# Early bias loads moved to another queue and place, constant products ahead of the first projection, and two blocks of squares issued later, in a two-layer hybrid decoder trunk

## The chip, the cores and the metric

The kernel runs on one core of one Trainium2 chip. The metric is the device time of one execution in microseconds; lower is better. Engines are named as in the profile: PE is TensorE's matrix products, PEld its weight loads, DVE is VectorE, ACT ScalarE, POOL GpSimd, SP SyncE, which issues most of the DMA transfers.

## The reference

Input x is (1, 256, 2048) float32, and so is the output. Two layers; each is a mixer and a SwiGLU feed-forward, both with an RMS norm ahead and a residual add behind; a final RMS norm follows. Weights are float32.

```python
def reference(x, ...):
    h = x
    for layer in range(2):
        xn = rms_norm(h, norm_mix[layer])
        if layer % 2 == 0:
            # one projection feeds two groups of heads: sliding-window attention
            # (16 q heads, 4 kv heads of 64, window 128, ALiBi, sinks) and
            # mLSTM (4 heads, input gate and forget gate with biases b_i, b_f)
            mix = swa_mlstm_mixer(xn, w_in_even, w_out_even, swa_sinks, mlstm_b_i, mlstm_b_f, head_gain)
        else:
            # causal attention with 16 heads of 128 and a cumulative log forget gate (bias fox_b_f)
            mix = forgetting_attention_mixer(xn, w_in_odd, fox_b_f, w_out_odd)
        h = h + mix
        h = h + swiglu(rms_norm(h, norm_ffn[layer]), w_gate[layer], w_up[layer], w_down[layer])
    return rms_norm(h, norm_final)

def rms_norm(x, g):
    return x * lax.rsqrt(jnp.mean(x * x, axis=-1, keepdims=True) + 1e-5) * g
```

## The kernel before, in words

**Products.** Every float32 operand of a large product is split into a rounded part and a rest: `hi` and `lo` for weights, `xh` and `xl` (or `mh` and `ml`) for activations, which stand transposed, with the model dimension on the partitions. One product is then three: `hi` with `xh`, `lo` with `xh`, `hi` with `xl` (lines 184 to 186 in `gemm`, 405 to 407 in `three`).

**Weights** come in chunks of 256 rows by up to 512 columns: `load_raw` issues the transfer on SyncE's queue (line 112), into one of four buffers; `split_chunk` rounds it to `hi` on ScalarE (line 156) and subtracts on VectorE for `lo` (line 157). A chunk feeds 12 products: two slices of 128 rows, two tiles of 128 tokens, three parts. `latest[0]` is the last cast, `load[0]` the last load issued. `tc.issue_after(ins)` puts all that is issued inside it behind `ins` on that engine's queue. Apart from that, the order on each engine's queue is planned when the kernel is built, by the order in the source and by when the planner expects operands to be there; each engine then works through its queue in order.

**The start.** SyncE's queue loads the transposed input `xc` (five transfers, line 122), interleaved with the first four weight chunks of k's projection, `ahead`. Pool writes constants (`ident`, `ones`, `upper`, `mhalf`) and issues four small loads, each a row of 4 or 16 floats copied to all 128 partitions: `bias_g` (lines 140 and 141), `sink` (143), `bias_f` (145). The tiles are read much later: `sink` in the attention of layer 0, `bias_g` at the mLSTM's gates, `bias_f` at layer 1's gates.

The first projection is k and v of the sliding-window attention (eight chunks): ScalarE makes `xh` from `xc` with the norm's gain (line 689), VectorE `xl` (line 690), four slices at a time, then `gemm` runs over them. The norm's division is applied behind the product, by `r`. Then comes q's projection, eight chunks more, in four steps; with each step a quarter of the input `h` is loaded on SyncE's queue (line 700) and its squares summed on ScalarE (`square_sum`, line 207), for `r`.

**The seam from layer 0 to layer 1.** The feed-forward's last two output blocks (n = 2 and 3 of four blocks of 512 columns) are added to `h` by `close`; each is then turned for layer 1 in two steps that wait in the list `pending`. `start` issues a transposing DMA of the two halves of the words, `join` puts the halves together again (line 240, ScalarE), scales them to `xh` (line 262, ScalarE) and makes `xl` (line 263, VectorE). `first_values` runs the first products of layer 1 meanwhile, those that need only blocks 0 and 1 (k below 8, into `vacc0` and `tacc1`), then those of block 2 (k = 8 and 10), and takes a step from `pending` after four of them: both starts, the first join, and after `(0, 10)` the second. The squares of all four blocks, under the key `"m1"`, are summed in `close`, and `rstd("m1")` (lines 213 and 214 on VectorE, 216 on Pool) makes the norm's factor `r1` from them; it is first applied at line 1028.

Of the kernel before, what the change touches and what calls it, by code (L numbers as in the profile page):

```python
# [7 lines left out]
F32 = mybir.dt.float32  # L8
# [9 lines left out]
P = 128  # L18
# [14 lines left out]
OFF_QM, OFF_KM, OFF_VM, OFF_OM = 1536, 2048, 2560, 3584  # L33
CAP = 15.0
FILL = 24
ORDER = ((0, 0), (0, 1), (1, 2), (0, 3), (1, 4), (0, 5), (1, 6), (0, 7))
DOWN = {
    6: ((0, 0), (0, 1), (1, 2), (0, 3), (1, 4), (0, 5)),
# [14 lines left out]
def mixed_of(order):  # L53
    return [p for w, p in order if w]
# [5 lines left out]
def trunk(  # L60
# [20 lines left out]
    nc = tc.nc  # L81
# [8 lines left out]
    cp = ctx.enter_context(tc.tile_pool(name="cp", bufs=1))  # L90
    sm = ctx.enter_context(tc.tile_pool(name="sm", bufs=2))
    fill = ctx.enter_context(tc.tile_pool(name="fill", bufs=1)).tile([P, FILL], F32, name="fill")
    nc.gpsimd.memset(fill[:, 0:8], 0.0)
    pa = ctx.enter_context(tc.tile_pool(name="pa", bufs=4, space=PSUM))
    pm = ctx.enter_context(tc.tile_pool(name="pm", bufs=4, space=PSUM))
# [12 lines left out]
    load = [None]  # L108

    def load_raw(w, k0, c0, n, pool=wr, bufs=4):  # L110
        raw = pool.tile([P, CK, NB], F32, tag="raw", name="raw", bufs=bufs)
        load[0] = nc.sync.dma_start(
            raw[:, :, 0:n], w[k0 * P : (k0 + CK) * P, c0 : c0 + n].rearrange("(k p) n -> p k n", p=P)
        )
        return raw
# [5 lines left out]
    for k0, k1, ks in ((0, 2, (0,)), (2, 4, (2,)), (4, 8, (4, 6)), (8, 12, ()), (12, 16, ())):  # L121
        nc.sync.dma_start(xc[:, k0:k1, :], xt[:, k0:k1, :])
        ahead += [load_raw(wi, k, OFF_KS, NB) for k in ks]

    ident = cp.tile([P, P], F32, name="ident")
    nc.gpsimd.memset(ident, 0.0)
    nc.gpsimd.affine_select(
        out=ident, in_=ident, pattern=[[-1, P]], compare_op=ALU.not_equal, fill=1.0, base=0, channel_multiplier=1
    )
    ones = cp.tile([P, P], F32, name="ones")  # L130
    nc.gpsimd.memset(ones, 1.0)
    upper = cp.tile([P, P], F32, name="upper")
    nc.gpsimd.affine_select(
        out=upper, in_=ones, pattern=[[1, P]], compare_op=ALU.is_ge, fill=0.0, base=0, channel_multiplier=-1
# [2 lines left out]
    nc.gpsimd.memset(mhalf, -0.5)  # L137

    bias_g = cp.tile([P, 8], F32, name="bias_g")
    nc.gpsimd.dma_start(bias_g[:, 0:4], mlstm_b_i[0].partition_broadcast(P))  # L140
    nc.gpsimd.dma_start(bias_g[:, 4:8], mlstm_b_f[0].partition_broadcast(P))
    sink = cp.tile([P, SWA_H], F32, name="sink")
    nc.gpsimd.dma_start(sink, swa_sinks[0].partition_broadcast(P))
    bias_f = cp.tile([P, FOX_H], F32, name="bias_f")
    nc.gpsimd.dma_start(bias_f, fox_b_f[0].partition_broadcast(P))

    latest = [None]

    def load_chunk(w, k0, c0, n):
        raw = ahead.pop(0) if ahead else load_raw(w, k0, c0, n)  # L150
        return split_chunk(raw, n)
# [10 lines left out]
    def new_acc():  # L162
        return [pa.tile([P, NB], F32, tag="acc", name="acc") for _ in range(NT)]
# [6 lines left out]
    def gemm(acc, lhs, w, c0, n, k_from, k_to, k_all, skew=1):  # L170
        k0 = k_from
        while k0 < k_to:
            last = k_to == k_all and k0 + skew * CK >= k_all
            chunks = [load_chunk(w, kc, c0, n) for kc in range(k0, k_all if last else k0 + CK, CK)]
            order = [(i, t) for i in range(len(chunks) * CK) for t in range(NT)]
            if last:
                order.sort(key=lambda it: it[1])
            for i, t in order:
                k = k0 + i
                hi, lo = (c[:, i % CK, 0:n] for c in chunks[i // CK])  # L180
                ah, al = lhs(k)
                ts = slice(t * P, (t + 1) * P)
                o = acc[t][:, 0:n]
                nc.tensor.matmul(o, ah[:, ts], hi, start=(k == 0), stop=False)  # L184
                nc.tensor.matmul(o, ah[:, ts], lo, start=False, stop=False)  # L185
                nc.tensor.matmul(o, al[:, ts], hi, start=False, stop=(k == k_all - 1))  # L186
            k0 += len(chunks) * CK
# [14 lines left out]
    def square_sum(key, n):  # L202
        if n == 0:
            sums[key] = sm.tile([P, NT, 4], F32, tag="ss", name="ss")
        for t in range(NT):
            junk = sm.tile([P, NB], BF16, tag="junk", name="junk", bufs=1)
            nc.scalar.activation(
                junk, h[:, t, n * NB : (n + 1) * NB], AF.Square, accum_out=sums[key][:, t, n : n + 1]
            )
# [34 lines left out]
    def turn_scaled(room, idx, n, extra=None):  # L244
# [10 lines left out]
        def join():  # L255
# [10 lines left out]
            for half in range(2):  # L266
                pair = 2 * n + half
                if extra is None or pair not in mixed_of(ORDER):
                    continue
                m = mixed_of(ORDER).index(pair)  # L270

# [13 lines left out]
    def add_out(acc, n):  # L285
        for t in range(NT):
            o = h[:, t, n * NB : (n + 1) * NB]
            nc.vector.tensor_tensor(out=o, in0=acc[t], in1=o, op=ALU.add)
# [88 lines left out]
    def run_next(pending):  # L377
        if pending:
            with tc.issue_after(latest[0].ins):
                pending.pop(0)()  # L380
# [162 lines left out]
    def ffn(layer, fp, room, pending, sx, sd, key, idx_next=None, key_next=None, finish=None, then=None):  # L543
        r = rstd(key)

        def sums_x(pair):
            j = mixed_of(ORDER).index(pair)
            return sx[0][:, j, :, :], sx[1][:, j, :, :]

        for g0, g1 in zip(PARTS, PARTS[1:]):  # L550
# [5 lines left out]
            for g in range(g0, g1):  # L556
                par = (g1 - 1 - g) % 2
                plain, c = pair_group(
                    room, par, x_of, sums_x, [(w_gate[layer], g * NB), (w_up[layer], g * NB)], ORDER, todo
                )  # L560
# [60 lines left out]
            def close(acc, n):  # L621
                if not end:
                    add_out(acc, n)
                elif idx_next is None:
                    finish(acc, n, gf)
                else:
                    add_out(acc, n)
                    pending.extend(turn_scaled(room, idx_next, n))
                    square_sum(key_next, n)

            gf = None
            wd = w_down[layer][4 * g0 * P : 4 * g1 * P, :]
            for n0 in (0, 2):
                if end and idx_next is None and n0 == 2:
                    for n in (2, 3):
                        acc = new_acc()
                        gemm(acc, m_of, wd, n * NB, NB, 0, nk, nk, skew=3 if n == 3 else 1)
                        close(acc, n)
                    continue
# [22 lines left out]
                for m in range(2):  # L662
                    close(plain[m], n0 + m)
# [32 lines left out]
    acc1 = new_acc()  # L696
    for n in range(4):
        gemm(acc1, x_of, wi, OFF_QS, NB, 4 * n, 4 * n + 4, KT)
        with tc.issue_after(load[0].ins):
            nc.sync.dma_start(h[:, :, n * NB : (n + 1) * NB], xv[:, :, n * NB : (n + 1) * NB])  # L700
        square_sum("m0", n)
    r = rstd("m0")
    with tc.tile_pool(name="ev", bufs=1) as ev:
# [101 lines left out]
        acc = tacc  # L805
# [199 lines left out]
    late = ctx.enter_context(tc.tile_pool(name="late", bufs=1))  # L1005
    sx = [late.tile([P, len(mixed_of(ORDER)), 4, P], F32R, name=f"sx{i}") for i in range(2)]
    wi1 = w_in_odd[0]
# [7 lines left out]
    def first_values(pending):  # L1015
        for acc, c0, n, k0 in FIRST_ODD:
            gemm((vacc0, tacc1)[acc], x_of, wi1, c_v + c0, n, k0, k0 + 2, KT)
            if (acc, k0) in ((0, 4), (0, 6), (1, 4), (0, 10)):
                run_next(pending)

    close_layer(0, w_out_even[0], 2, "f0", begun=begun0, idx_next=1, key_next="m1", then=first_values)

    r1 = rstd("m1")
    with tc.tile_pool(name="od", bufs=1) as od:
# [8 lines left out]
        acc = tacc1  # L1033
# [120 lines left out]
    def finish(acc, n, gf):  # L1154
        ns = slice(n * NB, (n + 1) * NB)
        gn_ = gf[n // CK][:, n % CK, :]
        for t in range(NT):
            o = h[:, t, ns]
            nc.vector.tensor_tensor(out=o, in0=acc[t], in1=o, op=ALU.add)
            junk = sm.tile([P, NB], BF16, tag="junk", name="junk", bufs=1)  # L1160
            nc.scalar.activation(junk, o, AF.Square, accum_out=fs[:, t, n : n + 1])
            part, mean, rs = (ft[:, a, t : t + 1] for a in range(3))
            if n < 3:
                nc.vector.tensor_tensor(out=o, in0=o, in1=gn_, op=ALU.mult)
            if n == 2:
                nc.vector.reduce_sum(part, fs[:, t, 0:3], axis=AX)
                nc.vector.tensor_scalar(part, part, 1.0 / D, EPS, op0=ALU.mult, op1=ALU.add)
            if n < 3:
                continue
            nc.vector.tensor_scalar(mean, fs[:, t, 3:4], 1.0 / D, part, op0=ALU.mult, op1=ALU.add)  # L1170
            nc.gpsimd.tensor_tensor(out=rs, in0=mean, in1=mhalf[:, 0:1], op=ALU.pow)
            nc.scalar.mul(h[:, t, 0 : 2 * NB], h[:, t, 0 : 2 * NB], rs)
            nc.vector.tensor_scalar(h[:, t, 2 * NB : 3 * NB], h[:, t, 2 * NB : 3 * NB], rs, None, op0=ALU.mult)
            nc.vector.scalar_tensor_tensor(out=o, in0=o, scalar=rs, in1=gn_, op0=ALU.mult, op1=ALU.mult)
            for half in (1, 0):
                hs = slice(half * 2 * NB, (half + 1) * 2 * NB)
                nc.sync.dma_start(ov[:, t, hs], h[:, t, hs])
# [51 lines left out]
```

## Time and profile before

| | |
|---|---|
| median of 3 runs | 2106.6 us (2105.95 to 2106.67) |
| the profiled execution's own time | 2107.07 us |
| its span | 2105.4 us |
| granted TensorE clock, mean | 0.998 |
| TensorE (PE) busy | 99% of the span, 9558 products |
| VectorE, ScalarE, Pool busy | 86%, 63%, 2% |
| DMA | 429.33 MB, mean 204 GB/s |

The profile is one execution, and the times in it are microseconds from the start of its span. Idle time of an engine says what it waited for. A DMA share of 1 means that all 16 DMA engines are full.

### The profile page before, as it was taken

What the parts mean: (1) busy time and instruction counts of PE and PEld (TensorE: products, weight loads), DVE (VectorE), ACT (ScalarE), POOL (GpSimd) and SP (SyncE); (2) the same over time, 40 slices, a digit from 0 to 9 for tenths busy, and PEclk for the clock granted to TensorE, in tenths of its full rate; (3) what the DMA queues carried; (4) which work ended last, traced back from release to release, by engine and by line L of the source; (5) the groups of instructions that cost most, each with busy time, mean ns of one, the idle gap of its engine ahead of it and who ended that gap; (6) DMA issues with size and microseconds to landing.
All of it is one profiled execution on the core that took longest, in us unless ns stands there. A gap on an engine that the chain in (4) does not pass through costs nothing.

```text
span 2105.4 us, 26803 instructions
## 1 busy us (share of the span) xinstructions
PE 2085.8 (99%) x9558; PEld 1729.8 (82%) x9558; DVE 1819.2 (86%) x2402; ACT 1324.4 (63%) x1685; POOL 50.3 (2%) x74
## 2 busy tenths in 40 slices
PE   8999999999999999999999999999999999999998
PEld 6878888888888888888888888888888888888886
DVE  6688758998999999998888878669989999998995
ACT  6565568665577646667865556586755677556763
POOL 2100000000000000000000000000000000000000
PEclk9999999999999999999999999999999999999999
DMA  9446667766677657666775655577756677667763
GB/s 321 122 139 182 225 195 221 240 194 197 197 223 224 219 193 226 205 219 179 197 252 175 180 178 164 179 221 229 242 170 222 216 212 218 210 191 227 217 209 126
DMA packets 282870, 429.33 MB, mean 204 GB/s; under 512 B 80448, under 2 KB 88688, under 8 KB 282736
## 3 DMA queue, kind: packets, MB, share of 16 engines
q1 hardware_dynamic: 280848, 421.78, 64.6%
q0 software_dynamic: 1744, 5.81, 1.0%
q8 instruction: 75, 1.23, 0.2%
q14 instruction: 59, 0.48, 0.1%
q10 hardware_dynamic: 144, 0.03, 0.0%
HBM read 408.67 MB, written 2.11 MB: 195 GB/s over the span
## 4 chain that ended last, share of the span: by engine, by line
PE 91%; DVE 4%; DMA 2%; issue 1%; ACT 1%; SPq 0%; POOLq 0%; POOL 0%; DVEq 0%; ACTq 0%
PE acc L405 19%; PE acc L406 19%; PE acc L407 19%; PE acc L186 5%; PE acc L185 5%; PE acc L184 5%; PE prod L405 5%; PE prod L406 5%; PE prod L407 5%; DVE lo L157 2%; DMA raw<-in_w_up_dram 1%; PE vacc L186 1%; PE vacc L184 1%; PE vacc L185 1%; PE ptm L294 1%
## 5 line engine op out<-in xcount | busy, mean ns | idle before, releaser
L156 ACT CAST hi<-raw 128x1024 fp32r<-128x1024 f32 (+1 forms) x664 | 675.0, 1031 | 461.6 <-PE acc L407 228.2
L157 DVE TENSOR_TENSOR lo<-raw,hi 128x1024 fp32r<-128x1024 f32 (+1 forms) x664 | 784.6, 1196 | 141.5 <-ACT hi L156 139.9
L406 PE MATMUL acc<-lo,xh 128*128 128x512 f32 x1207 | 470.3, 390 | 0.5 <-DVE lo L157 0.5
L407 PE MATMUL acc<-hi,xl 128*128 128x512 f32 x1207 | 467.3, 389 | 0.0
L405 PE MATMUL acc<-hi,xh 128*128 128x512 f32 x1207 | 465.4, 390 | 1.5 <-DVE u L537 0.9
L405 PEld LDWEIGHTS acc<-hi,xh 128*128 128x128 f32 x1207 | 226.5, 188 | 50.4 <-DVE u L537 1.9
L406 PEld LDWEIGHTS acc<-lo,xh 128*128 128x128 f32 x1207 | 226.6, 188 | 47.6 <-DVE lo L157 0.7
L407 PEld LDWEIGHTS acc<-hi,xl 128*128 128x128 f32 x1207 | 226.6, 188 | 47.1
L406 PE MATMUL acc<-lo,mh 128*128 128x512 f32 x444 | 172.8, 389 | 0.0
L407 PE MATMUL acc<-hi,ml 128*128 128x512 f32 x444 | 171.3, 390 | 0.0
L405 PE MATMUL acc<-hi,mh 128*128 128x512 f32 x444 | 169.7, 389 | 0.0
L282 ACT CAST ht<-t 128x1024 fp32r<-128x1024 f32 x94 | 98.9, 1052 | 54.3 <-PE prod L407 46.9
L282 ACT CAST ht<-raw 128x1024 fp32r<-128x1024 f32 x94 | 98.8, 1051 | 44.2 <-PE acc L407 17.2
L184 PE MATMUL acc<-hi,mh 128*128 128x512 f32 x320 | 126.2, 395 | 0.0
L185 PE MATMUL acc<-lo,mh 128*128 128x512 f32 x320 | 124.9, 390 | 0.0
L186 PE MATMUL acc<-hi,ml 128*128 128x512 f32 x320 | 124.8, 392 | 0.0
L283 DVE TENSOR_TENSOR lt<-raw,ht 128x1024 fp32r<-128x1024 f32 x94 | 114.4, 1217 | 9.5 <-ACT ht L282 9.2
L282 ACT CAST hi<-raw 128x512 fp32r<-128x512 f32 (+1 forms) x115 | 72.4, 630 | 76.1 <-PE acc L407 65.3
L283 DVE TENSOR_TENSOR lt<-t,ht 128x1024 fp32r<-128x1024 f32 x94 | 114.3, 1216 | 6.1 <-ACT ht L282 6.0
L405 PEld LDWEIGHTS acc<-hi,mh 128*128 128x128 f32 x444 | 83.3, 188 | 17.3
L406 PEld LDWEIGHTS acc<-lo,mh 128*128 128x128 f32 x444 | 83.3, 188 | 17.3
L407 PEld LDWEIGHTS acc<-hi,ml 128*128 128x128 f32 x444 | 83.4, 188 | 17.2
(386 smaller groups left out, 3548.4 us busy)
## 6 DMA issues: line engine op xcount, KB each, us to landing
raw<-in_w_gate_dram SPq DMA_DIRECT2D x176, 512.0 KB, 4.6
raw<-in_w_up_dram SPq DMA_DIRECT2D x176, 512.0 KB, 4.7
raw<-in_w_down_dram SPq DMA_DIRECT2D x176, 512.0 KB, 4.8
raw<-in_w_in_odd_dram SPq DMA_DIRECT2D x88, 512.0 KB, 4.5
raw<-in_w_in_even_dram SPq DMA_DIRECT2D x64, 512.0 KB, 4.6
raw<-in_w_out_even_dram SPq DMA_DIRECT2D x32, 512.0 KB, 4.2
raw<-in_w_out_odd_dram SPq DMA_DIRECT2D x32, 512.0 KB, 4.6
raw<-in_w_in_odd_dram SPq DMA_DIRECT2D x8, 272.0 KB, 3.1
```

The costliest lines, as they stand in the source:

```text
L156: latest[0] = nc.scalar.copy(hi[:, :, 0:n], raw[:, :, 0:n])
L157: nc.vector.tensor_tensor(out=lo[:, :, 0:n], in0=raw[:, :, 0:n], in1=hi[:, :, 0:n].bitcast(F32), op=ALU.subtract)
L184: nc.tensor.matmul(o, ah[:, ts], hi, start=(k == 0), stop=False)
L185: nc.tensor.matmul(o, ah[:, ts], lo, start=False, stop=False)
L186: nc.tensor.matmul(o, al[:, ts], hi, start=False, stop=(k == k_all - 1))
L282: nc.scalar.copy(dst_h, src)
L283: nc.vector.tensor_tensor(out=dst_l, in0=src, in1=dst_h.bitcast(F32), op=ALU.subtract)
L294: nc.tensor.transpose(pt[:, i, :], s_, ident)
L405: nc.tensor.matmul(o, ah, hi, start=start, stop=False)
L406: nc.tensor.matmul(o, ah, lo, start=False, stop=False)
L407: nc.tensor.matmul(o, al, hi, start=False, stop=stop)
```

## The change

Three edits. The tile `ones` is written first, and twelve products of it with itself, `WARM` = 3 groups of four 128x128 float32 products into a PSUM tile that nobody reads, stand ahead of everything on TensorE. The four small loads leave Pool's queue; `small_loads` issues them on SyncE's queue in the second step of q's projection, behind that step's last weight load and ahead of the load of `h`. At the seam, `close` sums only the squares of blocks 0 and 1; those of blocks 2 and 3 are issued in `first_values`, behind the cast of chunk `(0, 10)` on ScalarE's queue.

```diff
+WARM = 3
...
+    ones = cp.tile([P, P], F32, name="ones")
+    nc.gpsimd.memset(ones, 1.0)
+    for _ in range(WARM):
+        pw = pm.tile([P, 4, P], F32, tag="pm", name="pw")
+        for i in range(4):
+            nc.tensor.matmul(pw[:, i, :], ones, ones, start=True, stop=True)
     ident = cp.tile([P, P], F32, name="ident")
     nc.gpsimd.memset(ident, 0.0)
...
-    ones = cp.tile([P, P], F32, name="ones")
-    nc.gpsimd.memset(ones, 1.0)
...
     bias_g = cp.tile([P, 8], F32, name="bias_g")
-    nc.gpsimd.dma_start(bias_g[:, 0:4], mlstm_b_i[0].partition_broadcast(P))
-    nc.gpsimd.dma_start(bias_g[:, 4:8], mlstm_b_f[0].partition_broadcast(P))
     sink = cp.tile([P, SWA_H], F32, name="sink")
-    nc.gpsimd.dma_start(sink, swa_sinks[0].partition_broadcast(P))
     bias_f = cp.tile([P, FOX_H], F32, name="bias_f")
-    nc.gpsimd.dma_start(bias_f, fox_b_f[0].partition_broadcast(P))
+
+    def small_loads():
+        nc.sync.dma_start(bias_g[:, 0:4], mlstm_b_i[0].partition_broadcast(P))
+        nc.sync.dma_start(bias_g[:, 4:8], mlstm_b_f[0].partition_broadcast(P))
+        nc.sync.dma_start(sink, swa_sinks[0].partition_broadcast(P))
+        nc.sync.dma_start(bias_f, fox_b_f[0].partition_broadcast(P))
...
                     pending.extend(turn_scaled(room, idx_next, n))
-                    square_sum(key_next, n)
+                    if n < 2:
+                        square_sum(key_next, n)
...
         gemm(acc1, x_of, wi, OFF_QS, NB, 4 * n, 4 * n + 4, KT)
+        if n == 1:
+            with tc.issue_after(load[0].ins):
+                small_loads()
         with tc.issue_after(load[0].ins):
             nc.sync.dma_start(h[:, :, n * NB : (n + 1) * NB], xv[:, :, n * NB : (n + 1) * NB])
...
             gemm((vacc0, tacc1)[acc], x_of, wi1, c_v + c0, n, k0, k0 + 2, KT)
+            if (acc, k0) == (0, 10):
+                with tc.issue_after(latest[0].ins):
+                    square_sum("m1", 2)
+                    square_sum("m1", 3)
             if (acc, k0) in ((0, 4), (0, 6), (1, 4), (0, 10)):
                 run_next(pending)
```

## The prediction

> **What bounds the kernel now.** I read the page first, then TensorE's waits over the whole run, then the chain that ended last, and only then the two places the change touches.
>
> ```profile
> span 2105.4 us, 26803 instructions
> PE 2085.8 (99%) x9558; PEld 1729.8 (82%) x9558; DVE 1819.2 (86%) x2402; ACT 1324.4 (63%) x1685; POOL 50.3 (2%) x74
> ```
>
> TensorE is busy for 2085.8 of 2105.4 us. Nothing that the change leaves alone can move the time by much, so what counts is where TensorE stands still or runs slowly. Its waits (engine, line, whom it waited for: us in total, times, longest):
>
> ```profile
> PE acc L184 <- ACT hi L156: 6.7, 1, 6.7
> ...
> PE vacc L184 <- ACT xh L262: 0.5, 1, 0.5
> PE vacc L186 <- DVE xl L263: 0.4, 1, 0.4
> PE acc L185 <- DVE lo L157: 0.2, 1, 0.2
> ```
>
> The first and the last of these lie at the kernel's start, the two `vacc` waits at the seam from layer 0 to layer 1: the two places where something is edited. At the start, TensorE's clock and the data both matter. Rows of the timeline (start, length, engine, line, what; `x2` is two instructions merged; in brackets the idle time before):
>
> ```profile
> 6.72 1.22 PE L184 MATMUL acc<-hi,xh 128*128 128x512 f32 x2 [6.72 <-ACT hi L156]
> 12.41 1.03 PE L184 MATMUL acc<-hi,xh 128*128 128x512 f32 x2
> 13.74 0.39 PE L185 MATMUL acc<-lo,xh 128*128 128x512 f32 x1
> 13.97 0.39 PE L186 MATMUL acc<-hi,xl 128*128 128x512 f32 x1
> 16.37 0.50 PE L185 MATMUL acc<-lo,xh 128*128 128x512 f32 x1 [0.19 <-DVE lo L157]
> 16.41 3.31 ACT L689 ACTIVATE xh<-xc,gT 128x256 fp32r<-128x256 f32 x8 [0.23 <-DMA xc<-in_xt_dram]
> 19.63 1.98 ACT L156 CAST hi<-raw 128x1024 fp32r<-128x1024 f32 x2
> 20.69 5.23 DVE L157 TENSOR_TENSOR lo<-raw,hi 128x1024 fp32r<-128x1024 f32 x4
> 21.97 0.50 PE L185 MATMUL acc<-lo,xh 128*128 128x512 f32 x1
> ```
>
> A chunk of weights is 12 products. Chunk 1 runs from 6.72 to 12.41 us, 5.69 us; at the later spacing of 0.23 us (13.74 to 13.97) it would be 2.7 us. TensorE is at half pace until about 13 us. Chunk 3's `lo` arrives only at 16.37, and chunk 5's at 21.97, behind eight `xh` (ScalarE, from 16.41, when an `xc` landed), a cast (19.63) and a subtraction (20.69). Between 22 and 60 us TensorE waits for nothing, so the first `lo` of chunk 5 sets the start of everything behind it. Up to it 50 products are issued (four chunks and two L184): 50 x 0.227 = 11.4 us in 15.25 us. **3.9 us is all that the start can lose or give back beyond its first wait.** The chain of waits says who holds it:
>
> ```profile
> 2.73 9.66 DMA xc<-in_xt_dram
> 12.41 1.71 ACT xh L689 x4
> ```
>
> So the transfers do: a 512 KB load issued at 2.73 us lands after 9.66 us.
>
> **Small loads away from the start.** Busy times by stretch (from:to, length, then PE, PEld, DVE, ACT, POOL, granted clock, DMA share, GB/s), and the DMA queues of the first 22 us (q0 is Pool's queue):
>
> ```profile
> 5.00:11.00 6.00, 4.24 (x9) 2.94 (x10) 2.70 (x5) 2.51 (x5) 0.00 (x0) 1.00 0.95 230
> 11.00:20.00 9.00, 8.81 (x34) 6.76 (x34) 7.82 (x14) 7.85 (x16) 0.00 (x0) 1.00 1.04 400
> ...
> q1 hardware_dynamic: 2904, 6.31, 80.5%
> q0 software_dynamic: 128, 0.02, 9.2%
> q10 hardware_dynamic: 144, 0.03, 0.7%
> ```
>
> Four loads with 0.02 MB between them hold 9.2% of 22 us, 2.0 us of every DMA engine. While they run the engines are as full as later (0.95 against 1.04) but move 230 instead of 400 GB/s: (400 - 230) x 6 = 1.02 MB short, 2.55 us at 400 GB/s. Without them all that is queued behind lands 2.0 to 2.55 us earlier; I take 2.3, between the two readings. `xc` for the eight `xh` then comes at 14.1 instead of 16.41, and with the same work behind it chunk 5's `lo` at 19.7 instead of 21.97.
>
> **Idle products.** TensorE must also get there by 19.7. With the clock as now, chunk 1 ends at 12.41 again; about 0.3 us for the last slow products, then 36 products of 0.227 us (8.2) and two L184 (0.45) lead to 21.35: only 0.6 us of the 2.3. At full pace, chunk 1 ends near 10.3, chunk 2 (its `lo` 2.3 us earlier) near 13, chunk 3's `lo` comes at 14.1, and 22 products and two L184 lead to 19.5, inside 19.7. So the data are worth 0.6 us alone, the clock alone nothing (the `lo` of 16.37 and 21.97 stay), and the two together 2.3 us. The nearest row for an idle product is a 128x128 float32 product of the mLSTM part, 16 instructions for eight products:
>
> ```profile
> L923 PE MATMUL pq<-qmt,kmt x16: 272/275/275, 198.1 to 199.8; 128*128 128x128 f32 x16
> ```
>
> (199.8 - 198.1) / 15 = 0.113 us per instruction, 0.227 per product, at half pace 0.45: twelve take 2.7 to 5.4 us. Their operand is written by one Pool memset, now the first of its tile work, at about 1 us, so they lie between about 1.2 and 6.6 us, inside the first wait of 6.72 us. They cost nothing; at the slow end they finish just as the first `hi` does. The Trainium skill, "TensorE: Matmul & The Clock Gate", Part 1, says that the clock is halved until a window of some 3.4 us, which runs free of the kernel, has been busy throughout; this trace agrees (full spacing 6 us after the first product, with gaps in the first window), and by it twelve products just suffice, or fall short by one window when the phase is bad.
>
> **The small loads' new place.** They go to SyncE's queue behind chunk 12's load and ahead of a load of `h`: four more issues in order. What they meet there (first DVE, then PE rows are chunk 9 and chunk 13):
>
> ```profile
> 26.37 0.51 SPq L700 DMA_DIRECT2D h<-in_x_dram  x1
> 31.66 1.55 SPq L112 DMA_DIRECT2D raw<-in_w_in_even_dram  x2
> ...
> 30.22 2.60 DVE L157 TENSOR_TENSOR lo<-raw,hi 128x1024 fp32r<-128x1024 f32 x2 [4.30 <-ACT hi L156]
> 32.99 0.39 PE L185 MATMUL acc<-lo,xh 128*128 128x512 f32 x1
> 39.50 2.58 DVE L157 TENSOR_TENSOR lo<-raw,hi 128x1024 fp32r<-128x1024 f32 x2 [0.25 <-ACT hi L156]
> 43.87 0.39 PE L185 MATMUL acc<-lo,xh 128*128 128x512 f32 x1
> ```
>
> Issue: 4 x 0.51 = 2.0 us, in a hole of SyncE's queue from 26.9 to 31.66. Transfer: between 0.6 us (four times what ScalarE's one load, q10 above, holds: 0.7% of 22 us) and the 2.0 us that they hold now. Pool's queue loses four issues; at 2% busy it gates nothing here. Behind them stand that `h`, its squares on ScalarE, and chunk 13, whose `lo` ends at 39.5 + 1.3 = 40.8 and is needed at 43.87: 3.1 us of cover, more than the 2.0. Chunk 9, with the thinner cover of 1.5 us (30.22 + 1.3 against 32.99), is loaded ahead of them and moves with the start. I take 0; without the cover it would be up to 2.0 us. The skill's "DMA: Bandwidth & Descriptors", "Issuing engines are not separate DMA queues", speaks against this edit: whoever issues, the loads run on the same 16 DMA engines. By it the 2.0 us of engine time is moved, not saved; without cover the start would net 0.3 us, which no row here supports.
>
> **The seam.** ScalarE, DVE and TensorE in time around it:
>
> ```profile
> 1034.48 0.63 ACT L207 ACTIVATE junk<-h 128x512 bf16<-128x512 f32 x1
> 1037.54 0.63 ACT L207 ACTIVATE junk<-h 128x512 bf16<-128x512 f32 x1
> 1039.10 2.58 ACT L240 COPY c<-turned 128x1024 uint16<-128x1024 uint16 x2
> 1041.55 0.62 ACT L207 ACTIVATE junk<-h 128x512 bf16<-128x512 f32 x1
> 1042.17 2.94 ACT L156 CAST hi<-raw 128x1024 fp32r<-128x1024 f32 x3
> 1045.01 1.71 ACT L262 ACTIVATE xh<-c,gT 128x256 fp32r<-128x256 f32 x4
> 1042.30 0.16 DVE L213 TENSOR_REDUCE tot<-ss 128x2 f32<-128x8 f32 x1 [1.84 <-ACT junk L207]
> 1050.10 1.72 ACT L262 ACTIVATE xh<-turn,gT 128x256 fp32r<-128x256 f32 x4
> 1060.45 1.26 ACT L1028 ACTIVATE vn<-vacc,r 128x512 f32<-128x512 f32 x2
> 1045.57 0.50 PE L184 MATMUL vacc<-hi,xh 128*128 128x512 f32 x1 [0.54 <-ACT xh L262]
> 1047.18 0.73 PE L186 MATMUL vacc<-hi,xl 128*128 128x512 f32 x2 [0.42 <-DVE xl L263]
> ```
>
> From 1034.48 on ScalarE works without a hole, and three squares (0.62 us each, 1.9 in all) stand ahead of the `xh` that TensorE waits for. Taken away, that `xh` can come 1.9 us earlier and both stalls (0.54 + 0.42 = 0.96) go. But the squares are not dropped: they are released after the cast of the last chunk ahead of the second join. If all four (2.5 us) come between that cast and L262, `xh` is 0.6 us later than now. So the seam lies between -0.96 and +0.6; I take -0.8, nearer the gain, because the second join's copies (1039.10) can start a good half microsecond earlier and need none of the squares. The root that the squares feed is first used at 1060.45 us, far behind.
>
> **Sum.** -2.3 (start) + 0 (products) + 0 (loads in q's projection) - 0.8 (seam) = -3.1 us: 2104.0 for the profiled execution, whose own time is 2107.07 (its span and 1.7 us around it); from the median of 2106.6 it is 2103.5. Measurements of this kernel tell apart about 0.2%, 4.2 us: below 2102.4 counts as faster, above 2110.8 as slower.
>
> **Rivals.** *All of it comes back.* The start gives its whole 3.9 us (chunk 1's data early as well) and the seam 0.96: -4.9, 2101.7. For it: the shortfall of 1.02 MB may understate what the loads held up. Against: `xh`, cast and subtraction of chunk 5 remain in series. Chance 0.22.
>
> *The clock does not come free in time*, or the loads are not what slowed the first 11 us. Then the start gives 0 to 0.6 and the seam 0.8: -1.4 at best, 2105.2. For it: the twelve products may end a little before the first real one, and in the trace of before a window with gaps did not suffice. The page named above would allow this in a bad phase. Chance 0.22.
>
> *Slower: VectorE is held by the reduction of the squares.* VectorE's queue is in order, and already now it stood 1.84 us at L213 for a square. If the squares run behind both joins, they begin after the last `xh` (1050.10 + 1.72) and end 2.5 us later, at 1054.3. If L213 kept its place at 1042, the `xl` that TensorE takes at 1047.18 would wait until then and TensorE with it, 7.1 us: -2.3 + 7.1 = +4.8, 2111.4. It decides only if L213 stays ahead of `xl` in VectorE's queue; the order is planned anew, and nothing needs the root before 1060 us. Chance 0.11, with other reorderings of that kind.
>
> **How the numbers follow.** The forecast itself has 0.45, and covers 2102.5 to 2104.8 (start 2.0 to 2.55, seam -0.96 to +0.2). The range reaches to the first two rivals, 2101.3 to 2107.5, and leaves out the slower one and the far side of the first. Faster by over 0.2%: 0.22; slower by over 0.2%: 0.11; within: 0.67.
>
> **What would show it.** Right: float32 products of a constant tile from about 1.2 us; the first chunk's twelve products in about 3.5 us instead of 5.69; 5 to 11 us moving well above 300 GB/s; the `xc` of 16.41 at about 14.1 and the L185 of 21.97 at about 19.7; no TensorE wait near 40 us; the two `vacc` waits gone. Wrong: the 230 GB/s stays without Pool's loads; the early spacing stays 0.43; a new wait of TensorE on `lo` between 35 and 50 us; DVE waiting long at L213.

## The result, and the profile after

The changed kernel takes 2102.19 us (median of 22 runs, 2099.36 to 2105.2), the kernel before 2106.12 us (22 runs on the same chip, 2103.59 to 2109.5). The ratio is 0.998, 95% interval 0.9974 to 0.9987: 3.9 us less, with an interval of about 2.7 to 5.5 us. That is 0.19%, just inside the 0.2% that the prediction took as the least that can be told apart, but the interval leaves out zero. The forecast was -3.1 us. The profiled execution took 2100.61 us, 6.5 us less than the profiled one of before; where the other 2.6 us are from is shown below.

In the changed kernel the lines stand a little lower down: the cast is L163, the subtraction L164, the first projection's products L191 to L193, its `xh` L697, the squares L214, their reduction L220, the joins L247, L269 and L270. First the page, and TensorE's waits over the whole run (us in total, times, longest):

```profile
span 2098.9 us, 26844 instructions
...
PE 2085.3 (99%) x9582; PEld 1732.6 (83%) x9582; DVE 1818.7 (87%) x2402; ACT 1325.4 (63%) x1685; POOL 45.6 (2%) x70
...
PE pw L131 <- POOL ones L127: 1.1, 1, 1.1
PE prod L412 <- ACT mh L289: 1.1, 2, 0.6
PE acc L412 <- DVE c L545: 1.0, 2, 0.8
PE acc L192 <- DVE lo L164: 0.5, 1, 0.5
```

Both `vacc` waits are gone, and the 6.7 us wait for the first `hi` has become 1.1 us for `ones`: the twelve idle products now stand in it as busy time, which is why TensorE's busy time has hardly fallen although the run is shorter. Now the start, TensorE's timeline and then ScalarE's, and the busy times by stretch:

```profile
1.10 5.20 PE L131 MATMUL pw<-ones 128*128 128x128 f32 x24 [1.10 <-POOL ones L127]
6.65 0.73 PE L191 MATMUL acc<-hi,xh 128*128 128x512 f32 x2 [0.35 <-ACT hi L163]
7.91 0.50 PE L192 MATMUL acc<-lo,xh 128*128 128x512 f32 x1 [0.53 <-DVE lo L164]
10.31 0.62 PE L191 MATMUL acc<-hi,xh 128*128 128x512 f32 x2
...
19.12 0.49 PE L192 MATMUL acc<-lo,xh 128*128 128x512 f32 x1
...
13.53 3.31 ACT L697 ACTIVATE xh<-xc,gT 128x256 fp32r<-128x256 f32 x8 [0.22 <-DMA xc<-in_xt_dram]
...
5.00:11.00 6.00, 5.12 (x23) 3.91 (x23) 4.30 (x8) 4.58 (x9) 0.00 (x0) 1.00 1.04 385
26.00:40.00 14.00, 14.00 (x64) 11.59 (x63) 8.05 (x7) 10.02 (x17) 1.68 (x5) 1.00 0.99 354
```

The idle products end at 6.30, and the first real one starts at 6.65, 0.07 us earlier than in before. Chunk 1 takes 3.66 us (6.65 to 10.31) instead of 5.69. From 5 to 11 us the transfers move 385 GB/s instead of 230. The `xc` of 16.41 is there at 13.53, and chunk 5's first `lo` product starts at 19.12 instead of 21.97: 2.85 us earlier. That difference stays within 0.2 us of this until a stretch near 150 us, of which more below.

A part of the shift is already there when SyncE issues its transfers. The last two `xc`, first in before, then in the changed kernel:

```profile
6.09 2.25 SPq L122 DMA_DIRECT2D xc<-in_xt_dram  x2
```

```profile
4.29 1.02 SPq L123 DMA_DIRECT2D xc<-in_xt_dram  x2
```

So with the small loads on Pool's queue, SyncE came to these two issues 1.8 us later and took 1.2 us longer over them. Whether this late issue makes the transfer late, or is only another effect of the full DMA engines, was not tried.

At the seam, ScalarE, then VectorE, then TensorE:

```profile
1036.03 0.62 ACT L214 ACTIVATE junk<-h 128x512 bf16<-128x512 f32 x1
...
1037.69 1.70 ACT L269 ACTIVATE xh<-c,gT 128x256 fp32r<-128x256 f32 x4
...
1040.24 0.63 ACT L214 ACTIVATE junk<-h 128x512 bf16<-128x512 f32 x1
...
1047.67 0.64 ACT L214 ACTIVATE junk<-h 128x512 bf16<-128x512 f32 x1
...
1049.20 0.15 DVE L220 TENSOR_REDUCE tot<-ss 128x2 f32<-128x8 f32 x1
...
1039.63 0.40 PE L191 MATMUL vacc<-hi,xh 128*128 128x512 f32 x1
```

One square is left ahead of the first join's `xh`, the other three come behind it. That `xh` starts 1.94 us ahead of the product that uses it (1037.69 against 1039.63); before, the product stood waiting for it and started 0.56 behind it (1045.01 and 1045.57). Now it starts without a wait. The reduction moved behind the joins, to 1049.20. Compared product by product, TensorE's lead over before grows by 1.5 us here.

The two profiled executions differ in other places as well. In before's, TensorE's clock was halved for a while near 150 us, and there was a wait at 426 us; the rows are before's, and then the changed kernel's for the first of them (TensorE alone: from:to, length, busy, clock, DMA share, GB/s):

```profile
150.00:160.00 10.00, 10.00 (x38) 0.84 0.17 52
...
426.38 0.50 PE L405 MATMUL acc<-hi,xh 128*128 128x512 f32 x1 [0.95 <-DVE u L537]
```

```profile
150.00:160.00 10.00, 10.00 (x45) 1.00 0.27 65
```

The slow stretch costs 1.55 us and the wait with its restart 1.24; a longer wait in the changed kernel's profile (`c`, at 531 us) gives 0.57 back. So -2.85 (start) -1.55 -1.24 +0.57 -1.5 (seam) = -6.57, the 6.5 us between the two profiles. Start and seam alone make -4.35, inside the interval of the medians. The slow stretch comes and goes from run to run (last section). Whether the wait at 426 us belongs to every execution of the kernel before cannot be read from its one profile. None of the other twelve profiles has it, on lines that no edit touched. With it the sum would be -5.6, just beyond the interval of 2.7 to 5.5 us, so the medians speak against counting it.

### The profile page after: what moved, and what is told of

Read it like the earlier page. It is cut to its first block, busy times and chain, and to the rows that moved or that the text cites. A ratio compares the mean times of both kernels' runs of the same rounds, so it can differ in the third digit from the quotient of the medians.

```text
span 2098.9 us, 26844 instructions
## 1 busy us (share of the span) xinstructions
PE 2085.3 (99%) x9582; PEld 1732.6 (83%) x9582; DVE 1818.7 (87%) x2402; ACT 1325.4 (63%) x1685; POOL 45.6 (2%) x70
## 4 chain that ended last, share of the span: by engine, by line
PE 92%; DVE 5%; issue 1%; DMA 1%; ACT 1%; POOLq 0%; POOL 0%; SPq 0%; DVEq 0%; ACTq 0%
PE acc L413 19%; PE acc L412 19%; PE acc L414 19%; PE acc L193 5%; PE acc L192 5%; PE acc L191 5%; PE prod L412 5%; PE prod L414 5%; PE prod L413 5%; DVE lo L164 2%; PE vacc L193 1%; PE vacc L192 1%; PE vacc L191 1%; DMA raw<-in_w_up_dram 1%; PE ptm L301 1%
## 5 line engine op out<-in xcount | busy, mean ns | idle before, releaser
L163 ACT CAST hi<-raw 128x1024 fp32r<-128x1024 f32 (+1 forms) x664 | 675.2, 1031 | 462.1 <-PE acc L414 223.3
L164 DVE TENSOR_TENSOR lo<-raw,hi 128x1024 fp32r<-128x1024 f32 (+1 forms) x664 | 785.8, 1198 | 137.0 <-ACT hi L163 135.0
L191 PE MATMUL acc<-hi,mh 128*128 128x512 f32 x320 | 126.3, 396 | 0.0
L193 PE MATMUL acc<-hi,ml 128*128 128x512 f32 x320 | 125.0, 393 | 0.0
```

Of the source, the lines that this page charges most:

```text
L163: latest[0] = nc.scalar.copy(hi[:, :, 0:n], raw[:, :, 0:n])
L164: nc.vector.tensor_tensor(out=lo[:, :, 0:n], in0=raw[:, :, 0:n], in1=hi[:, :, 0:n].bitcast(F32), op=ALU.subtract)
```

## The experiments

The theory is the prediction's: small loads and clock together give the start, each of them alone little; a cover hides the loads at their new place; the seam is squares ahead of an `xh`. "Lead" is the start of TensorE's n-th product in the kernel before minus that in the kernel named, both from the profiles.

### Each part alone

From before: `w_only` adds the twelve products, `l_only` moves the loads, `wl` does both, `s_only` moves the squares.

```diff
# w_only
+WARM = 3
+    for _ in range(WARM): ...            # the products of ones, as in the change
# l_only
-    nc.gpsimd.dma_start(bias_g[:, 0:4], mlstm_b_i[0].partition_broadcast(P))   # and three more
+        if n == 1:
+            with tc.issue_after(load[0].ins):
+                small_loads()
# s_only
-                    square_sum(key_next, n)
+                    if n < 2:
+                        square_sum(key_next, n)
...
+            if (acc, k0) == (0, 10):
+                with tc.issue_after(latest[0].ins): ...   # the squares of blocks 2 and 3
```

> Before plus the idle products alone. Data-and-clock theory (neither edit of the start gives much without the other): chunk 1 runs at the short spacing of 0.23 us, but chunk 3 still waits for its lo until about 16.4 us and chunk 5 for its lo until about 21.97 us, so TensorE only idles more; total within 0.3 us of before. Rival (the clock carries the gain): chunk 5's first lo product at about 19.1 to 20 us and a total 2 to 2.8 us below before.

> Before plus the moved small loads alone. Data-and-clock theory: the xc that eight xh wait for lands at about 13.5 instead of 16.4 us and chunk 5's lo is ready near 19 us, but TensorE, at half pace until about 13 us, takes it only at about 21.3 us: total about 0.6 us below before. Rival (the data carry the gain): first lo product of chunk 5 at about 19.1 us, total about 2.8 us below before. Second rival (the slow transfers of the first 11 us are not the small loads' doing): xc lands at 16.4 us as before.

> Idle products and moved loads, squares where they were before. Data-and-clock theory: first lo product of chunk 5 at about 19.1 us, 2.85 us earlier than before, and that lead kept up to the seam; there the two waits of 0.54 and 0.42 us on xh and xl are as before. Total about 2.8 us below before. Rival (the lead is lost in q's projection, where the small loads stand now): a wait of TensorE between 30 and 60 us and a total less than 2 us below before.

> Before with only the squares of blocks 2 and 3 moved. Seam theory: the start as before (21.97 us); the two TensorE waits on xh and xl at the seam gone; TensorE gains about 1.5 us across the seam (the two waits and the slower issue around them), total about 1.5 us below before. Rival (the squares only change places with other ScalarE work): the waits stay or move to the next xh, total within 0.5 us of before. Second rival (the gain comes from TensorE's changed order after the seam): the lead still grows after 1053 us by more than 0.3 us.

| kernel | median us | ratio to before (2106.34), 95% interval | lead at chunk 5's first `lo`, us | growth at the seam, us |
|---|---|---|---|---|
| `w_only` | 2105.5 | 0.9997 (0.9989 to 1.0006) | 0.5 | -0.8 |
| `l_only` | 2106.39 | 1.0 (0.999 to 1.0009) | 1.4 | -0.2 |
| `wl` | 2104.53 | 0.9988 (0.998 to 0.9997) | 3.1 | none |
| `s_only` | 2104.32 | 0.9989 (0.998 to 0.9998) | 0.3 | 1.5 |

Here is `w_only`, then `l_only`, then the pace of the products in `s_only`, whose start is that of before:

```profile
15.89 3.31 ACT L694 ACTIVATE xh<-xc,gT 128x256 fp32r<-128x256 f32 x8 [0.22 <-DMA xc<-in_xt_dram]
...
21.49 0.47 PE L190 MATMUL acc<-lo,xh 128*128 128x512 f32 x1
```

```profile
13.69 3.31 ACT L691 ACTIVATE xh<-xc,gT 128x256 fp32r<-128x256 f32 x8 [0.23 <-DMA xc<-in_xt_dram]
...
10.66 0.53 PE L187 MATMUL acc<-lo,xh 128*128 128x512 f32 x1
11.03 0.39 PE L188 MATMUL acc<-hi,xl 128*128 128x512 f32 x1
...
20.58 0.39 PE L187 MATMUL acc<-lo,xh 128*128 128x512 f32 x1
```

```profile
11.30 0.40 PE L185 MATMUL acc<-lo,xh 128*128 128x512 f32 x1
11.53 0.40 PE L186 MATMUL acc<-hi,xl 128*128 128x512 f32 x1
```

With the clock alone, chunk 5's `lo` product comes 0.48 us earlier (21.49), about as much as `xc` landed earlier in this run (15.89 against 16.41). Even `s_only`, with nothing changed at the start, is 0.25 us earlier there. So the clock alone gives nothing that stands out, and the data hold the start. With the loads alone, `xc` lands 2.7 us earlier, and the product 1.4 us: TensorE at half pace takes the rest. The forecast had 0.6 here, because it kept the slow products to 13 us; in this run the pace is full from about 11 us. That is not the moved loads' doing: in `s_only` it is full from 11.3 us too (11.30 to 11.53, 0.23 us). The time varies from run to run, and 0.6 or 1.4 is luck.

At the seam `w_only` loses 0.8 us, because its wait for the `xh` there is 1.3 us instead of 0.54, on lines that the edit did not touch; why was not followed. Neither edit alone is measurable in the medians. The two together are: 3.1 us in the profile, 1.8 us in the medians (interval 0.6 to 4.2). With the squares' 2.0 us it makes 3.8 of the whole change's 3.9 us. Within these wide intervals the start and the seam add up. That the two edits at the start depend on each other is shown by the profiles (0.5 and 1.4 alone, 3.1 together); the medians are too coarse for it.

### How many idle products

From `wl`: `WARM` is 1 (four products) and 6 (twenty-four), one time each.

```diff
-WARM = 3
+WARM = 1          # warm1; 6 in warm6
```

> Idle products and moved loads, squares as before, but one group of four idle products instead of three: about 1.1 to 2.9 us, then TensorE idles until the first chunk. Theory (the products must fill one window of the clock gate, some 3.4 us, and only then is the clock free for the first chunk): the clock comes free only at 10 to 13.6 us, chunk 1 runs at 0.43 us a product, and chunk 5's first lo product lies at 20.3 to 21.3 us, as in the kernel with the moved loads alone (20.58 us). Rival (any early product is enough): clock free before 8 us and that product at about 18.7 to 19.1 us.

> The same with six groups, 24 idle products. Theory (twelve products fit in the first wait, more do not): half pace until 5 to 7.6 us, then 0.23 us a product, so they end at about 8.8 to 9.5 us, the first real product starts 2 to 3 us later than at 6.6 us, and chunk 5's first lo product comes at 20.2 to 21 us instead of 18.7 to 19.1. Rival (the transfers hold the start alone and hide the products): that product at about 19 us.

Measured: 2106.16 and 2103.29 us, before 2105.18 us beside them; single times say little here, as runs of one kernel lie up to 6 us apart. The profiles say more. First `warm1`, then `warm6`, then `wl` itself:

```profile
1.10 2.08 PE L131 MATMUL pw<-ones 128*128 128x128 f32 x8 [1.10 <-POOL ones L127]
6.63 1.22 PE L191 MATMUL acc<-hi,xh 128*128 128x512 f32 x2 [3.46 <-ACT hi L163]
...
12.24 0.62 PE L191 MATMUL acc<-hi,xh 128*128 128x512 f32 x2
...
20.87 0.39 PE L192 MATMUL acc<-lo,xh 128*128 128x512 f32 x1
```

```profile
1.10 7.84 PE L131 MATMUL pw<-ones 128*128 128x128 f32 x48 [1.10 <-POOL ones L127]
8.70 0.71 PE L191 MATMUL acc<-hi,xh 128*128 128x512 f32 x2
...
20.15 0.39 PE L192 MATMUL acc<-lo,xh 128*128 128x512 f32 x1
```

```profile
18.89 0.43 PE L192 MATMUL acc<-lo,xh 128*128 128x512 f32 x1
```

After four products with a gap of 3.46 us behind them, chunk 1 runs at half pace (6.63 to 12.24, 5.61 us), and chunk 5's `lo` product stands at 20.87. With twelve it is 18.89. Twenty-four run on into the first chunk, whose products start 2.05 us later than in the changed kernel (8.70 against 6.65); 1.3 us of it are left at chunk 5 (20.15 against 18.89). So the number matters on both sides, and of the three numbers tried, twelve end closest ahead of the first `hi`. The Trainium skill, "TensorE: Matmul & The Clock Gate", Part 1, with its rule of a free-running window of some 3.4 us that has to be busy throughout, agrees: 2.08 us of products freed nothing, 5.20 us did.

The stretch rows print a clock of 1.00 over the whole start, also where the products run at half pace. The trace has no record of the clock before the first one of a full clock, and that one fits the pace: it stands at 13.3 us in before, 10.9 in `l_only`, 11.3 in `s_only` and 12.1 in `warm1`, but at 7.3 in `w_only`, 4.9 in `wl`, 5.9 in the changed kernel and 5.8 in `warm6`.

### Whose time the small loads take

From `wl`: `sp_early` issues the four loads on SyncE's queue at the start, behind the last `xc`; `pool_late` leaves them on Pool's queue, behind its later load of `gain`. From the whole change: `no_small` leaves them out.

```diff
# sp_early
+    small_loads()
+
     latest = [None]
# pool_late (nc.gpsimd.dma_start in small_loads)
+        g_load = nc.gpsimd.dma_start(gain, mlstm_head_gain[0].partition_broadcast(P))
+        with tc.issue_after(g_load.ins):
+            small_loads()
# no_small
+    nc.gpsimd.memset(bias_g, 0.0)        # and sink, bias_f; small_loads is empty
```

> Idle products, squares as before, and the small loads on SyncE's queue but at the start, behind the last xc and ahead of chunk 5's weights. It tells the queue from the place. Theory 'Pool's packets are slow' (on Pool's queue each held an engine for 0.6 to 1 us; on SyncE's queue, in q's projection, a row took about 0.01 us and they cost little): no stretch at 230 GB/s, the last xc lands at about 13.5 us, chunk 5's first lo product at 18.7 to 20.2 us. Theory 'the place is at fault' (small rows at the start cost the same from any queue): 200 to 250 GB/s for several microseconds, and that product at 20.7 us or later.

> Idle products, squares as before, and the small loads on Pool's queue but late, behind the load of gain at about 18 to 21 us, beside the weights of chunks 9 to 12. Theory 'Pool's packets are slow wherever they stand': q0's 128- and 512-byte packets again hold hundreds of ns each, the rate falls for some microseconds between 21 and 32 us, and since chunks 9 and 11 have a cover of only 1.5 to 1.8 us, a TensorE wait of up to 1 us may come between 28 and 40 us. Theory 'only the start has no cover': the same slow packets, and no TensorE wait at all: first lo product of chunk 5 at 18.7 to 19.1 us and the lead kept. Third possibility (the packets were slow only because the engines were then starting up): packets of under 0.1 us.

> The changed kernel with the four small loads left out altogether (their tiles are filled with zeros by Pool, so biases and sinks count as zero). Theory (behind chunk 12 the loads are hidden whole by a cover of 2 to 3 us): TensorE has no wait between 20 and 60 us in the changed kernel and gets none here; the spacing to it stays within 0.2 us from 20 us to the seam, and the median within 1 us of the changed kernel's 2102.2; only the rate between 26 and 40 us rises, from 354 GB/s to 380 or more. Rival (a part of the 2.3 us still gets through, by a later cast or by the load of h): TensorE gains 0.5 to 2.3 us between 30 and 60 us, and the median falls to 2100 to 2101.5.

Measured: `sp_early` 2105.04 and `pool_late` 2103.91 us, one time each (before 2105.18); `no_small` a median of 2101.44 us (before 2106.28; ratio 0.998, 0.997 to 0.9989). First `sp_early` (busy times by stretch, ScalarE, SyncE's issues, TensorE), then the same issue of SyncE in the changed kernel (its x8 merges chunk 5 and those behind it), then `pool_late` (stretch, TensorE, ScalarE):

```profile
11.00:20.00 9.00, 8.19 (x37) 6.44 (x35) 6.71 (x13) 6.36 (x12) 2.54 (x7) 1.00 0.78 290
...
13.13 3.31 ACT L698 ACTIVATE xh<-xc,gT 128x256 fp32r<-128x256 f32 x8 [0.23 <-DMA xc<-in_xt_dram]
18.53 1.05 ACT L165 CAST hi<-raw 128x1024 fp32r<-128x1024 f32 x1 [2.09 <-DMA raw<-in_w_in_even_dram]
...
10.59 4.63 SPq L113 DMA_DIRECT2D raw<-in_w_in_even_dram  x4
...
21.47 0.51 PE L194 MATMUL acc<-lo,xh 128*128 128x512 f32 x1 [1.11 <-DVE lo L166]
```

```profile
7.88 13.15 SPq L113 DMA_DIRECT2D raw<-in_w_in_even_dram  x8
```

```profile
26.00:40.00 14.00, 12.20 (x53) 9.48 (x52) 6.25 (x6) 8.45 (x14) 2.04 (x5) 1.00 0.97 317
...
31.45 0.73 PE L191 MATMUL acc<-hi,xh 128*128 128x512 f32 x2 [1.27 <-ACT hi L163]
32.71 0.50 PE L192 MATMUL acc<-lo,xh 128*128 128x512 f32 x1 [0.53 <-DVE lo L164]
...
30.35 1.04 ACT L163 CAST hi<-raw 128x1024 fp32r<-128x1024 f32 x1 [8.73 <-DMA raw<-in_w_in_even_dram]
```

On SyncE's queue at the start, the loads let `xc` pass (13.13 us in this run), but the next weights are issued at 10.59 us instead of 7.88, and arrive too late for chunk 5: ScalarE waits 2.09 us for them, its `lo` product stands at 21.47, and 2.3 us of the lead are lost. So SyncE's queue is no remedy in itself. Neither of the two theories held whole. `xc` was not delayed, as the first had it; the product came late, as the second had it. But the rate fell otherwise than on Pool's queue: there the DMA engines were busy (a share of 0.95 at 230 GB/s), here they stand idle for a part of the time (0.78 at 290).

On Pool's queue at about 20 us the loads meet chunk 9, the one with the thin cover of 1.5 us: ScalarE waits for its weights, TensorE for ScalarE, and 2.3 us of lead go between 31 and 34 us. That is more than the expectation's 1 us, and the packets are slow here too, as in before, where the 64 that carry the rows held an engine for 0.5 us each on the mean (0.45 here). Both times a place without enough cover costs 2.3 us. By the Trainium skill, "DMA: Bandwidth & Descriptors", "Issuing engines are not separate DMA queues", whoever issues, the loads run on the same DMA engines; that both runs lose 2.3 us agrees with it.

Now the place of the change, chunk 13's subtraction (VectorE) in `no_small`, then in the changed kernel, with TensorE's first use there:

```profile
36.28 2.54 DVE L165 TENSOR_TENSOR lo<-raw,hi 128x1024 fp32r<-128x1024 f32 x2 [0.27 <-ACT hi L164]
```

```profile
37.42 2.56 DVE L164 TENSOR_TENSOR lo<-raw,hi 128x1024 fp32r<-128x1024 f32 x2 [0.25 <-ACT hi L163]
...
41.04 0.39 PE L192 MATMUL acc<-lo,xh 128*128 128x512 f32 x1
...
31.00:34.00 3.00, 3.00 (x15) 2.47 (x14) 1.49 (x2) 2.48 (x4) 0.00 (x0) 1.00 0.78 226
```

The loads do cost something here: the rate falls to 226 GB/s between 31 and 34 us, and chunk 13's `lo` comes 1.1 us later than without them (TensorE, too, runs 0.25 us earlier in `no_small`, from the start on, so about 0.9 us of it is theirs). Its first half is done by 38.7, and TensorE takes it at 41.04: 2.3 us of cover are left. TensorE waits for nothing. The median of `no_small` alone decides nothing: 2101.44 lies in the ranges of both the theory and the rival. The lead decides: between 25 and 100 us it grows by 0.01 us in `no_small` and by 0.03 in the changed kernel, where the rival asked for 0.5 or more. The rate between 26 and 40 us is 378 GB/s without the loads and 354 with them. The loads were issued from 23.75 us on, but the fall comes only at 31, and their packets of 16 and 64 bytes stand in the trace between 30.5 and 33.3 us. In SyncE's queue they take their turn behind the weights and `h` issued ahead of them, and so they come too late to meet chunk 9, whose first `lo` product starts at 30.16 us.

### Where the squares go

From the whole change: `sq_behind` issues the squares of blocks 2 and 3 behind the last `xh` of the second join; `sq_drop` has them not at all at the seam.

```diff
-            if (acc, k0) == (0, 10): ...              # in both
# sq_behind
+        with tc.issue_after(last_xh[0].ins):
+            square_sum("m1", 2)
+            square_sum("m1", 3)
# sq_drop (in close, for n < 2: reads block n, fills the sums of block n + 2)
+                        square_sum(key_next, n + 2, n)
```

> The changed kernel with the squares of blocks 2 and 3 issued on ScalarE behind the last xh of the second join, the place from which the prediction's slower rival counts. Rival: VectorE stands at the reduction of the squares (L213 of before) until the last square, about 1054, with the xl of the second join behind it; TensorE waits 5 to 7 us there, 2107 to 2109 in all. Theory (the reduction is planned where its operands are due, so it moves behind xl): no wait of TensorE above 0.3 us at the seam, its lead at the seam within 0.2 us of the changed kernel's, the reduction at 1052 to 1056, and the median within 1 us of 2102.2.

> The changed kernel with the squares of blocks 2 and 3 left out at the seam (those of blocks 0 and 1 are summed a second time in their place, early, in the feed-forward), which bounds what the place of the squares can give. Theory (the squares behind the cast cost nothing any more, and the two waits with what they carry are the whole 1.5 us): TensorE's lead over the kernel before grows by 1.5 us at the seam, as in the changed kernel, and the median is within 0.7 us of 2102.2. Rival (squares between the two joins still hold up the second xh): the lead grows by 1.9 us or more, the median is 2101.5 or less.

Measured (before 2106.28): `sq_behind` 2102.11 us, ratio 0.9979 (0.9969 to 0.9988); `sq_drop` 2105.43 us, 0.9998 (0.9988 to 1.0007). First `sq_behind`, then `sq_drop`:

```profile
1044.49 1.71 ACT L271 ACTIVATE xh<-turn,gT 128x256 fp32r<-128x256 f32 x4
...
1050.83 0.63 ACT L214 ACTIVATE junk<-h 128x512 bf16<-128x512 f32 x1
...
1045.35 1.67 DVE L272 SCALAR_TENSOR_TENSOR xl<-turn,gT,xh 128x256 fp32r<-128x256 f32 x4
...
1053.48 0.15 DVE L220 TENSOR_REDUCE tot<-ss 128x2 f32<-128x8 f32 x1
```

```profile
1300.56 0.73 PE L413 MATMUL prod<-mh,sx 128*128 128x512 f32 x2 [1.18 <-ACT mh L290]
```

With the squares behind both joins, the reduction simply moved along: to 1053.48, behind the second `xl` of 1045.35. TensorE does not wait at the seam. The lead grows by 1.6 us there, against 1.5 in the changed kernel, and the median is the same. The lead itself is 0.5 us smaller than the changed kernel's, where 0.2 was expected. That comes from the start, where it is 2.2 us instead of 2.85, as `xc` landed at 14.22 us in this run. The slower rival does not happen even in the place from which it counts. `sq_drop` also gains 1.5 us at the seam, so nothing more is to be had from the squares there. But its median misses the expectation by 3 us. It loses 0.8 us just ahead of the seam (one wait for a `lo` near 1003 us), and most of its lead in layer 1, between 1290 and 1330 us (1.18 us is the longest of the waits there), on lines that the edit did not touch. The order of the engines' queues is planned anew for each kernel, and this one came out worse there; why the plan differs there was not followed further. As a bound on the total, then, the experiment failed, and as a bound on the seam it stands.

## Why the prediction was right, and where its steps were off

**What bounds the kernel** was read rightly: both places where TensorE stood still or ran slowly gave time, and their sum in the profiles, -4.35, covers the medians' -3.9. The number owes something to luck all the same. Both terms were taken too small, and the median of 2102.2 lies just below the forecast's own 2102.5 to 2104.8; it lies inside the stated range because that reaches to the first rival.

**The start** was forecast at -2.3 us and is -2.85 in the profile; over the four profiles that have both edits there (the changed kernel, `wl`, `sq_behind`, `sq_drop`) it is -2.2 to -3.1. The mechanism is the one described: the data alone give something, the clock alone nothing, both together more than the sum. The term that was a little small is what the small loads hold up. The prediction put it between 2.0 us (the queue's busy time) and 2.55 us (the bytes short) and took 2.3; `xc` landed 2.88 us earlier (16.41 to 13.53). The time at which `xh` can begin varies from run to run: with the loads ahead of it, it was 15.89 to 16.41 in the three profiles that have them there, without them 13.13 to 14.22 in ten, on the mean 16.1 and 13.6. That is 2.5 us, so the byte count was the better of the two readings, and before's profile was a late one. With data alone, 0.6 was expected and 1.4 came, because the products' pace did not stay slow to 13 us. When it becomes full varies from run to run (10.9 to 13.3 us in the four kernels without enough early products), also where nothing at the start was changed; the prediction took before's one value as fixed.

**The idle products** cost nothing, as forecast. They took 5.20 us, the slow end of 2.7 to 5.4, and ended 0.35 us ahead of the first `hi`; in `w_only` they took 5.49, and the first real product stood at 6.64 all the same. The rival of a clock that does not come free was a live one: with four products it happens.

**The small loads' new place** is free for the reason given. The cost is 1.1 us of delay on chunk 13, inside "0.6 to 2.0", under a cover of about 3. The bound "up to 2.0 without cover" was low: the two places without cover lost 2.3 us. And the 2.0 us of engine time were not moved as they are: on SyncE's queue a packet took about 0.01 us, and what the loads cost there is the fall in the rate, with the DMA engines idle for a part of it (0.78 at 226 GB/s).

**The seam** was forecast at -0.8 and gives -1.5, below its lower bound of -0.96. That bound was the sum of the two bracketed waits, 0.54 + 0.42. But TensorE issued nothing for longer: its last product ahead of the first wait started at 1044.74, the next was due 0.13 us later and started at 1045.57, 0.70 us late; behind the second wait it is 0.58 (1046.60 due, 1047.18 started). The first spacing after each wait is also 0.1 us longer than usual (0.33 instead of 0.23). That makes 1.5. Two smaller faults: the copies at 1039.10 are those of the first join, not the second, and it is the first join's `xh` that TensorE waited for; and the case of a loss, with all four squares ahead of that `xh`, did not arise, since only one came ahead of it.

**The slower rival** was rightly given little: VectorE's reduction was planned behind `xl` in the changed kernel and in `sq_behind`. **The rival that all comes back** (-4.9) is closer to the profiles' -4.35 than the forecast of -3.1, and about as far from the medians' -3.9 as the forecast (1.0 and 0.8). It was right that the seam gives all of its waits, though its 0.96 was too small as well, and wrong about the start, where 3.9 us were never reached.

## What to carry to other kernels

Two causes that hide each other, here late data and a slow clock, have to be removed together: either one alone changed the median by less than its interval. A small load is free where its place in the queue puts it in front of something with cover, so look for the cover first and for the queue second. And the worth of a short wait is the gap between the starts of the products around it, less the usual spacing, not the idle time in its row.

## What the runs showed of the hardware that was not expected

TensorE's clock is halved for a stretch near 150 us in nine of the thirteen profiles, for 3.4 us, in `l_only` for 6.8; in `no_small` it happens once more, at 534 us. The kernels differ little or not at all there. In before it begins at 149.8 us, right behind a stretch of products with few rows and columns (4*128 and 4x4, 144 to 149 us). Near 150 us, 3.4 us of it cost about 1.5 us (1.55 in the profile of before), over a third of what the whole change gains. It is part of why single runs of one kernel differ by up to 6 us: of the 33 runs of before that were measured beside the four parts, the eight with a mean granted clock of 0.999 take 2104.7 us on the mean, the five with 0.997 2108.5. That the small products are the cause was not tried.

Small rows are dear beyond their bytes: four loads with 0.02 MB between them delayed what was queued behind them by 1.1 to 2.9 us, depending on the place. Their number of packets does not explain it either. On Pool's queue 64 packets of 128 and 512 bytes held an engine for 0.45 to 0.5 us each on the mean; on SyncE's queue there were 512, of 16 and 64 bytes, at about 0.01 us each, and the rate fell all the same. What sets the cost was not tried.
